# New issue orders for all five queues of a hybrid attention and DeltaNet layer

## The chip, the cores and the metric

The kernel runs on one core of one Trainium2 chip. The metric is the device time of one execution in microseconds (us), lower is better. Five engines work side by side and each takes its instructions strictly in order: TensorE (PE in the profile, PEld for its weight loads), VectorE (DVE), ScalarE (ACT), GpSimd (POOL) and SyncE (SP), which here does nothing but issue DMA transfers. POOL issues a few transfers too.

## What is computed

One layer of a diffusion backbone: 512 latent tokens and 256 context tokens, width 1024. Cut to what matters:

```python
hx = modulate(rms_norm(x), sh1, sc1); hc = modulate(rms_norm(ctx), csh1, csc1)
ak_x, av_x, qkv_x, db_x, da_x, aq_x, z_x, gate_x = split_cols(hx @ w_in)   # 512 tokens
ak_c, av_c, qkv_c, db_c, da_c = split_cols(hc @ w_in[:, :CTX_COLS])        # 256 tokens
attn = latent_attention(rope(norm(aq_x)), [k_c; k_x], [v_c; v_x])          # 8 heads, 768 keys
gdn  = gated_delta_net(silu(conv3(qkv)), decays, betas)   # 8 heads, both directions, chunked scan,
                                                          # a triangular solve in every chunk
y = (sigmoid(g_a) * (attn @ w_pa) + sigmoid(g_d) * (gdn @ w_pd)) @ w_out
x = x + g1 * y
x = x + g2 * (silu(g) * val) @ w_down   # g, val = conv3(modulate(rms_norm(x)) @ w_up)
return rms_norm(x, final_norm_w)
```

The modulations (sh1, sc1, g1, sh2, sc2, g2) are a vector times the 1024x6144 matrix w_mod.

## The kernel before

Every large product is made with three matmuls: each operand is split into a high part (rounded to fp32r) and a low part (what is left), and high x high, low x high and high x low are summed in one PSUM bank. ScalarE makes the high part of a weight tile (`whi<-wraw`), VectorE the low part (`wlo<-wraw,whi`); the raw tile (`wraw`, two buffers) comes from HBM by a transfer that SyncE issues. A column of a projection is 128 output channels: 8 x 3 matmuls into one of two banks called `mb` (`mc` in the second half of the kernel).

The work runs in this order. To about 53 us: the first modulations and norms. To 145 us: the projections for attention (`pq`). To 300 us: the attention, with projection columns of the DeltaNet woven between. From 300 to 729 us: the DeltaNet, head pair by head pair (four pairs), with more projection columns, and later the columns of w_pa and w_pd, woven in as filling; small matmuls of the scan write banks called `pb`. From 729 to 780 us the columns of w_pd alone, then w_out, and from about 830 us the MLP (`mc`).

For each head pair there is a triangular solve, 31 steps of two instructions (`prod<-X,R` and `R<-R,prod`), on VectorE for the first pair and on GpSimd for the other three; its result is transposed by VectorE into two tiles, `o_tr` and `o_nt`. The scan of a pair multiplies masks `M` (loaded as `M<-gamdr`, a constant added by GpSimd as `M<-M,cst`, then `M<-pqk,M` on VectorE) with `dl` on PE (`pb<-dl,M`).

The columns of w_pa are finished by `finish_pa`. For each of the eight columns it does a load, a multiplication and a store, through two buffers:

```python
def finish_pa(c, pa):
    ga = atA.tile([P, 512], F32, name="ga", tag="gt", bufs=2)
    SP.dma_start(ga, tdr[c])
    stt(ga, ga, 1.0, pa, ALU.add, ALU.mult)
    SP.dma_start(tdr[c], ga)
```

So the load of column c can be issued only when the store of column c-2 has landed, the multiplication waits for that load and for the column's bank `pa` (one of the two `mb`), and the bank is free for another column after the multiplication. The first two columns of w_pd take the two banks next; they read the DeltaNet's heads (`g_s`, `g_n`, `g_k`, `g_m`), of which four are reloaded (`sz<-gdr`) and split again. In the same stretch `late_mods` loads 24 rows of w_mod on GpSimd's queue into two buffers (`wl<-in_w_mod_dram`, 512 KB each), and VectorE multiplies each (`wl<-wl,cw`).

Every instruction of the kernel is recorded by one helper (line 275), which gives it a number in the order in which the program makes it, one count for each engine. At the end one string for each engine (`V_ORDER` for VectorE, `A_ORDER` ScalarE, `G_ORDER` GpSimd, `S_ORDER` SyncE, `T_ORDER` PE) lays down the order in which the queue holds them:

```python
def arrange(self, text):
    to = []
    for part in text.split():
        a, _, b = part.partition("-")
        to += [self.made[i].ins for i in range(int(a), int(b or a) + 1)]
    for a, b in zip(to, to[1:]):
        tc.add_manual_dep(b, a.name, ...)     # b stays behind a in its queue
```

An entry such as `1036 1038-1041` stands for five instructions. The waits between engines follow from the tiles that are read and written and are not laid down by the strings. These entries are spoken of below:

- SyncE: loads of `ga`, columns 4 to 7: 224, 227, 230, 233; stores `tdr<-ga`, columns 2 to 5: 217, 222, 225, 228; `sz<-gdr`: 214, 215, 219, 220; w_pa's last column of weights: 232; w_pd's first and second: 235, 236.
- VectorE: the multiplications of `ga`, columns 2 to 7: 1109, 1128, 1144, 1164, 1182, 1203; `g_s<-sz,g_s`: 1107, 1102; `wl<-wl,cw`: 1132; the low part of the weights for column 5 of w_pa: 1145; the last three R steps of the first pair's solve: 627, 629, 631, with `prod` 628, 630; the bank reads `t<-mb,col,t` behind them: 659, 660; `o_nt` of the second pair: 787, two of the `t<-mb,col,t` before it: 805, 806; a `KL<-pt,KH` of the attention's keys: 171.
- ScalarE: four copies out of a transposed bank, `co<-xb,hk`: 416 to 419; four copies `C<-NN`: 411 to 414; an exponential of the attention, `pm<-pS`: 253; a `whi<-wraw`: 315; a `TTm<-pb`: 503.
- GpSimd: the copy `TTm<-o_tr` 293 and the row load `wl<-in_w_mod_dram` 298.
- PE: the transposes `pt<-cst,qt` 634 and 635; the scores `pS<-KH,QH` 1454; `pb<-vtok,TTm` 2670; the first matmul of w_pd's second column, 4431.

Of the kernel before, what the change touches and what calls it, by code (L numbers as in the profile page):

```python
# [70 lines left out]
V_ORDER = ('2 6 5 0-1 3-4 7-65 70 66 71 67-68 72 75-76 78 77 73 79-80 82 74 83-84 81 120 69 85 92 86 91 87 93 89 '  # L71
           '88 94 90 95 100 96 102-103 97 99 98 104 101 105 121 111 122 106 112-114 124 107 115-116 125 117 123 '
           '128 119 108-110 126-127 130-131 129 136-137 118 134-135 132-133 139 138 187 141 158 142 159-161 165 '
           '162 166 163 167-169 188 164 143-145 170-176 178 146-148 179 177 149-150 222 180-183 151 190 184 152 '
           '191-192 140 189 153-155 193 156 194 185 157 223 197-198 186 195 199-202 196 204-205 203 220 214 '
           '206-208 255 215 209 211-212 210 213 224 216-219 256 225 232 226-230 287 233-234 240-241 235-237 221 '
           '231 242-244 238 245-248 305 249 253 250-251 336 239 252 257-259 265 260-261 254 262-263 266-268 272 '
           '269 273 271 274-276 264 277 270 279-284 347 278 288-289 285 295 286 296 354 297 290 292 291 306-307 '
           '298 293-294 300 299 313 308 314 301 309 302-303 311 310 312 315 304 319-320 317 316 321 318 322 327 '
           '368 328 324-326 329 323 337-338 385 330-331 339 343 333 332 334 340 344 341 335 342 345 400 350-351 '  # L80
           '346 394 405 348 352 359-360 349 357 353 358 361 355 362 369-370 356 436 371 364 363 372 365-366 '
           '375-376 374 367 373 377-378 431 381-382 380 443 379 450 383 390-391 384 388-389 386-387 401 392-393 '
           '402 395-398 403 408-410 399 404 407 414 406 415 464 412 411 413 422 481 423 420 424 416-417 419 418 '
           '421 432-433 425-426 434 427-428 439 429 440 435 496 437 430 446-447 441 438 442 444-445 448-449 '
           '455-456 453 452 490 454 457 451 465 458-459 466 501 460 467-468 461-462 471-472 470 463 469 477 475 '
           '473 478 474 553 479 531 476 486-487 484 480 483 488 485 482 497 489 498 491-492 499 493-494 504-505 '
           '500 562 502 506 495 510 503 508 511-512 509 507 518-519 516-517 514 513 515 520 527-528 522 521 529 '
           '523 530 524 534-535 532-533 525 536-539 638 540-541 526 542-543 546 550 548 547 674 678 672 544 549 '
           '545 551 671 679 552 675-676 673 677 680 797-798 792 927 793 554-555 794 556-557 799-800 795-796 '
           '559-560 558 644 561 563 567 566 564-565 633-634 568-569 650 635-636 570-576 637 577 639-640 578-583 '  # L90
           '641-642 584-588 643 589 656 590-591 645-646 592-595 647-648 596-601 649 662 602-604 651-652 605-607 '
           '653-654 608-611 668 612 655 613-617 657-658 618-627 659 628-631 660-661 663-664 632 670 666-667 665 '
           '683 692 669 681-682 704 685 688-689 684 687 690 708 832 693 930 934 691 694 932 928 933 686 696 931 '
           '935 695 697 699-700 698 801 703 701 716 702 709 705 710 706 726 711-713 929 714 707 740 717 833 721 '
           '719 718 715 720 727 729 728 722 730 723-724 731 734 756 732-733 735-736 741 725 737 743 742 744-745 '
           '776 748 746 739 747 749-750 738 757 751 758 958 752 759-760 753 761 766 808 764 762 767-768 765 763 '
           '769 754 770 777 755 771 779 773-774 778 780 772 782 815 783 785 959 775 784 788-789 805-806 791 781 '
           '786-787 790 936 823 802 834 803-804 809 812 835 813 807 811 810 814 831 817 836 840 816 818 839 841 '
           '837 843 845 838 842 844 819 824 820-821 852 826-827 1073 822 1072 825 828-830 846-847 863 849 848 '
           '854 853 855-857 850 858 876 859 864 860 851 862 866 861 868-869 867 865 870 889 871 873-874 872 875 '  # L100
           '879 877 880-882 906 878 883 886 884-885 887 916 888 892 890 894-895 893 891 896 901 899 897-898 904 '
           '902-903 900 907 905 911 910 908 912-914 909 917 940 920 915 918 923 919 924 921 925 922 926 946 '
           '937-939 942 960-961 957 945 941 944 948 943 962 967 947 963 966 968 950 949 970 953 951 965 969 971 '
           '954 972 952 964 981 1186 955-956 1187 973 977-978 974 979 975 980 992 976 982-984 1001 985 988 986 '
           '990 989 991 994 1018 993 987 995-997 999 1002 998 1004 1003 1005 1037 1000 1006 1009 1007-1008 '
           '1010-1011 1019 1021 1020 1012 1022 1055 1023 1013 1024 1028 1026 1029 1031 1030 1025 1032 1027 1042 '
           '1035 1014 1047 1036 1038-1041 1048 1016 1043 1033 1044 1034 1045-1046 1060 1015 1049-1052 1054 1053 '
           '1068 1017 1056-1057 1069 1074-1075 1061 1059 1058 1076 1062 1079 1094 1077-1078 1080 1063-1064 1081 '
           '1070 1084-1085 1065 1083 1066 1071 1086 1067 1087-1088 1092 1082 1110 1091 1098 1100 1089 1101 1099 '
           '1095 1093 1129 1097 1090 1103 1105-1106 1104 1109 1108 1115 1117-1118 1116 1114 1111 1145 1112 1120 '  # L110
           '1123 1126 1096 1121-1122 1124-1125 1128 1132-1135 1130 1136 1143 1165 1131 1137 1140 1148 1138-1139 '
           '1146 1141-1142 1153 1144 1149-1151 1107 1152 1147 1170 1183 1175 1154 1159 1102 1155 1160 1156 1162 '
           '1127 1163 1157-1158 1200 1161 1168 1201 1113 1171-1174 1119 1169 1176 1210 1164 1177-1178 1180 1166 '
           '1179 1181 1167 1204 1218 1185 1184 1223 1182 1205 1202 1188-1189 1203 1228 1190 1192 1195 1191 1194 '
           '1193 1197 1199 1196 1198 1217 1206 1208 1207 1209 1211-1212 1238 1213 1222 1214 1233 1219 1227 1215 '
           '1232 1216 1239 1220 1244 1224-1225 1229 1245 1237 1230 1221 1243 1226 1249 1231 1234 1240 1235 1241 '
           '1253 1246 1236 1247 1242 1248 1257 1250-1251 1261 1252 1265 1254 1256 1258 1255 1269-1270 1260 1262 '
           '1259 1263 1271 1301 1266 1274 1267 1264 1272 1268 1302 1273 1275-1277 1303 1278 1281-1282 1279 1283 '
           '1280 1285 1284 1287 1289 1286 1288 1300 1290-1291 1299 1293 1295 1292 1336 1297 1294 1304 1298 1296 '
           '1305-1307 1309 1311 1308 1310 1313 1312 1315 1314 1317 1316 1319 1321 1354 1318 1320 1322 1353 1331 '  # L120
           '1337 1323-1324 1372 1371 1340 1329 1325 1330 1345 1348 1326-1328 1332 1338 1333-1334 1341 1355 1390 '
           '1335 1339 1342-1343 1389 1346 1358 1347 1363 1349 1344 1350 1356-1357 1366 1351 1359 1352 1373 1360 '
           '1376 1364 1361 1407 1365 1362 1408 1381 1367-1369 1384 1370 1374-1375 1377 1391 1378-1380 1382 1394 '
           '1383 1420 1399 1402 1392 1385-1386 1393 1387-1388 1409 1395-1397 1400 1398 1412 1401 1417 1410 '
           '1403-1405 1421 1413 1411 1406 1426 1414-1415 1429 1422 1416 1418 1434 1437 1423 1427 1419 1424 1428 '
           '1442 1425 1435 1445 1430-1432 1450 1438 1436 1439 1433 1440 1443 1453 1444 1446-1448 1458 1461 1441 '
           '1451-1452 1466 1454 1449 1455 1459 1469 1456 1460 1462-1464 1457 1474 1477 1467 1465 1468 1482 '
           '1470-1471 1475 1485 1472 1476 1473 1478 1490 1479-1480 1493 1481 1483 1498 1484 1491 1486 1501 1492 '
           '1487-1489 1506 1494-1495 1507 1496 1499 1502 1500 1508 1497 1503-1504 1513-1514 1505 1509-1510 1515 '
           '1511-1512 1520-1521 1516 1522 1527 1518 1528 1519 1517 1529 1523 1525 1534 1524 1530 1526 1535-1536 '  # L130
           '1541 1531-1533 1537 1542 1539 1538 1543 1548-1549 1544-1545 1550 1555 1546 1556 1540 1547 1557 '
           '1551-1552 1558 1553 1559-1560 1554 1561-1567 1570 1568-1569 1571-1581')
# [1803 lines left out]
```

## Time and profile before

| what | value |
|---|---|
| time, median of three runs | 1207.3 us (1206.34, 1207.3, 1210.89) |
| the profiled execution's own time | 1203.08 us |
| its span, first to last instruction | 1201.3 us |
| mean granted TensorE clock | 0.993 of full speed |
| PE busy | 1172.9 us |
| DVE, ACT, POOL busy | 820.8, 591.4, 257.8 us |
| DMA moved | 174.96 MB, mean 146 GB/s |

Busy time of PE counts overlapping matmuls once. A matmul is drawn longer than the pace at which matmuls follow each other, so that an engine can be drawn busy through a short wait; the idle times given are lower bounds. The clock is given as a share of full speed, 2.4 GHz; 0.5 is 1.2 GHz.

### The profile page before, as it was taken

The numbers are of one execution on the slowest core, as the hardware profiler recorded it, in microseconds if no ns is written. First come the engines' busy times: TensorE is split into PE (matmuls) and PEld (weight loads), VectorE is DVE, ScalarE is ACT, GpSimd is POOL, SyncE is SP. The second block draws the span as 40 slices with busy tenths as digits, with TensorE's granted clock in tenths as the row PEclk, the third lists the DMA queues.
The fourth block names the chain that finished last, engine by engine and source line by source line (L and its number), as shares of the span: only waits on it lengthen the run. The fifth ranks groups of instructions, "written<-read, shape, count | busy, mean of one in ns | idle before, by whom it ended". The sixth has DMA issues, their size and how long they took to land.

```text
span 1201.3 us, 20365 instructions
## 1 busy us (share of the span) xinstructions
PE 1172.9 (98%) x7781; PEld 1012.9 (84%) x7781; DVE 820.8 (68%) x1614; ACT 591.4 (49%) x1372; POOL 257.8 (21%) x333
## 2 busy tenths in 40 slices
PE   9999999999998999999999998999999999999996
PEld 6899989999887888898887786889888888888886
DVE  4758798788798868856576896657676566563233
ACT  3535588777566756735446423334444444342231
POOL 0211100101304686784663111000000000000000
PEclk9999999999999999999999998999999999999998
DMA  9423333232444535435347777653433232333332
GB/s 380 155 96 102 109 92 125 69 112 86 186 170 147 179 113 182 169 107 190 129 139 244 254 258 262 230 185 107 158 140 105 88 106 89 105 97 97 97 97 70
DMA packets 57633, 174.96 MB, mean 146 GB/s; under 512 B 6240, under 2 KB 8768, under 8 KB 56128
## 3 DMA queue, kind: packets, MB, share of 16 engines
q1 hardware_dynamic: 54080, 161.08, 39.2%
q0 software_dynamic: 3456, 12.58, 3.2%
q8 instruction: 61, 1.00, 0.4%
q14 instruction: 36, 0.29, 0.1%
HBM read 146.85 MB, written 26.79 MB: 145 GB/s over the span
## 4 chain that ended last, share of the span: by engine, by line
PE 82%; DVE 9%; DMA 4%; issue 3%; POOL 1%; ACT 1%; SPq 0%; POOLq 0%; DVEq 0%; ACTq 0%
PE mc L275 34%; PE mb L275 24%; PE pb L275 7%; PE pq L275 6%; PE ab L275 4%; PE pS L275 3%; PE pm L275 2%; PE xb L275 1%; DVE R L275 1%; DVE t L275 1%; DMA tdr<-ga 1%; DVE wlo L275 1%; DMA wl<-in_w_mod_dram 1%; DVE prod L275 1%; PE pt L275 1%
## 5 line engine op out<-in xcount | busy, mean ns | idle before, releaser
L275 DVE TENSOR_TENSOR wlo<-wraw,whi 128x1024 fp32r<-128x1024 f32 (+3 forms) x155 | 188.6, 1220 | 104.1 <-ACT whi L275 103.3
L275 ACT ACTIVATE whi<-wraw 128x1024 fp32r<-128x1024 f32 (+3 forms) x155 | 159.2, 1030 | 177.2 <-PE mc L275 93.9
L275 PE MATMUL mc<-h,whi 128*128 128x512 f32 (+1 forms) x752 | 219.3, 376 | 0.0
L275 PE MATMUL mb<-hxH,whi 128*128 128x512 f32 x384 | 162.0, 422 | 3.3 <-DVE t L275 3.3
L275 PEld LDWEIGHTS mc<-h,whi 128*128 128x128 f32 x752 | 138.0, 188 | 25.4
L275 PE MATMUL mb<-hxH,wlo 128*128 128x512 f32 x384 | 151.7, 395 | 0.1
L275 PE MATMUL mb<-hxL,whi 128*128 128x512 f32 x384 | 149.7, 393 | 0.0
L275 PE MATMUL mc<-h,wlo 128*128 128x512 f32 (+1 forms) x376 | 141.2, 376 | 0.0
L275 PE MATMUL mc<-a,whi 128*128 128x512 f32 (+1 forms) x396 | 111.0, 366 | 0.6 <-DVE x L275 0.6
L275 POOL TENSOR_TENSOR rc<-rc,mhalf 128x2 f32<-128x2 f32 x4 | 3.0, 745 | 437.3 <-DVE rc L275 437.3
L275 PEld LDWEIGHTS mb<-hxH,whi 128*128 128x128 f32 x384 | 72.8, 190 | 17.7 <-DVE t L275 3.4
L275 PEld LDWEIGHTS mb<-hxH,wlo 128*128 128x128 f32 x384 | 72.4, 189 | 16.9 <-issue 0.6
L275 DVE SCALAR_TENSOR_TENSOR u<-mc,col,u 128x511 f32<-128x511 f32 x88 | 64.3, 745 | 28.1 <-ACT u L275 27.7
L275 PEld LDWEIGHTS mc<-a,whi 128*128 128x128 f32 x396 | 71.6, 189 | 12.8 <-DVE x L275 0.8
L275 PEld LDWEIGHTS mb<-hxL,whi 128*128 128x128 f32 x384 | 72.9, 190 | 11.1 <-DVE hxL L275 0.5
L275 PEld LDWEIGHTS mc<-h,wlo 128*128 128x128 f32 x376 | 70.8, 188 | 12.9
L275 PE MATMUL mc<-a,wlo 128*128 128x512 f32 (+1 forms) x198 | 72.4, 365 | 0.0
L275 POOL TENSOR_TENSOR prod<-X,R 128x31 f32<-128x31 f32 (+15 forms) x93 | 55.4, 596 | 21.8 <-DVE f L275 12.7
L275 ACT ACTIVATE u<-mc,col 128x512 f32<-128x512 f32 x44 | 33.7, 772 | 46.5 <-PE mc L275 35.1
L275 DVE SCALAR_TENSOR_TENSOR t<-mb,col,t 128x511 f32<-128x511 f32 (+1 forms) x76 | 49.0, 646 | 9.9 <-ACT t L275 9.0
L275 PE MATMUL pq<-whi,hxH 128*128 128x256 f32 (+1 forms) x192 | 55.4, 289 | 0.0
L275 POOL TENSOR_TENSOR R<-R,prod 128x31 f32<-128x31 f32 (+15 forms) x93 | 53.7, 577 | 6.9
(322 smaller groups left out, 2747.5 us busy)
## 6 DMA issues: line engine op xcount, KB each, us to landing
wraw<-in_w_cm_dram SPq DMA_DIRECT2D x48, 512.0 KB, 3.8
wraw<-in_w_up_dram SPq DMA_DIRECT2D x44, 512.0 KB, 3.3
wl<-in_w_mod_dram POOLq DMA_DIRECT2D x24, 512.0 KB, 4.6
wm<-in_w_mod_dram SPq DMA_DIRECT2D x8, 1024.0 KB, 13.4
wraw<-in_w_down_dram SPq DMA_DIRECT2D x16, 512.0 KB, 3.6
wraw<-in_w_aq_dram SPq DMA_DIRECT2D x10, 512.0 KB, 3.5
M<-gamdr SPq DMA_DIRECT2D x8, 512.0 KB, 6.6
wraw<-in_w_pa_dram SPq DMA_DIRECT2D x8, 512.0 KB, 4.5
```

What stands on the lines that cost most here:

```text
L275: self.made.append(fn(*a, **k))
```

## The change

No instruction, tile or transfer is added or removed. The five strings are replaced by other permutations of the same numbers. From the first place that differs to the last, the strings rule the stretch from 53 to 899 us of the profiled execution. Counted by the smallest set of entries that would have to be taken out and put back elsewhere, 490 of VectorE's 1582 entries move, 380 of ScalarE's 1182, 49 of GpSimd's 329, 103 of SyncE's 358 and 944 of PE's 6638 (mostly in groups of three, one k-step). No entry of SyncE stands more than 9 places from where it stood, none of VectorE more than 29.

The lines of the strings that hold the entries above, before and after:

```diff
 S_ORDER
-'214-215 217 232 224 219-220 222 227 235 237 225 238 230 236 228 233 243 231 246 234 249 239-242 244 '
+'229 217 215 232 224 235 222 225 219 227 220 236 230 228 237-238 233 243 231 246 234 239 241 240 249 '
...
 V_ORDER
-'162 166 163 167-169 188 164 143-145 170-176 178 146-148 179 177 149-150 222 180-183 151 190 184 152 '
+'222 146-147 182-183 148 171 149-151 184 152 190 153 191 189 185 223 192 154 156 193-194 155 197 195 '
...
-'653-654 608-611 668 612 655 613-617 657-658 618-627 659 628-631 660-661 663-664 632 670 666-667 665 '
+'652 605-607 653-654 608-609 668 610-611 655 612-615 657 616 658 617-629 659-661 663-664 630 670 '
...
-'769 754 770 777 755 771 779 773-774 778 780 772 782 815 783 785 959 775 784 788-789 805-806 791 781 '
-'786-787 790 936 823 802 834 803-804 809 812 835 813 807 811 810 814 831 817 836 840 816 818 839 841 '
+'781 786 791 787 823 805 803 802 804 806 834 813 835 807 936 809 811 810 812 816 831 817 837 844 814 '
...
-'1095 1093 1129 1097 1090 1103 1105-1106 1104 1109 1108 1115 1117-1118 1116 1114 1111 1145 1112 1120 '
-'1123 1126 1096 1121-1122 1124-1125 1128 1132-1135 1130 1136 1143 1165 1131 1137 1140 1148 1138-1139 '
+'1124 1130 1125 1132 1145 1128 1133 1135 1134 1136 1143 1131 1137 1165 1138 1140 1148 1139 1146 '
...
-'1127 1163 1157-1158 1200 1161 1168 1201 1113 1171-1174 1119 1169 1176 1210 1164 1177-1178 1180 1166 '
+'1156-1157 1162-1163 1161 1158 1200 1168 1171-1173 1166 1174 1164 1201 1113 1176 1169 1167 1119 1210 '
...
 A_ORDER
-'315 237 239 244 253 251 317 250 318-319 298 252 325 257 264 324 259 238 258 260-261 270 262-263 277 '
+'317 310 237 315 251 239 325 244 253 298 324 238 319 250 252 257 264 259-261 258 262 270 263 277 269 '
...
-'391-393 384 394-395 397-408 432 409 413 411-412 415 414 416-419 602 601 443 423 420 597 421 424 600 '
+'388 390 375 391 376 392 384 393-395 397-406 408 432 409 407 411-413 416 415 417-418 414 419 602 420 '
...
-'494 535 500 498 501 507 505 502 504 510 503 508 511 506 595 541 593 603 536 512 538 513 537 606 539 '
+'491 519 492 496-497 488 493-494 528 495 500 535 498 486 504 501 508 505 507 506 502 511 595 510 541 '
+'503 605 593 592 536 596 538 537 512 591 513-514 606 539 533 515 604 607 553 594 563 542 540 516 534 '
...
 G_ORDER
-'294 289-290 292 291 295 299-300 296 301 297-298 293 302-313 315-321 314 322-328')
+'222-285 289 294 290 293 291 295 299-300 292 301 297 296 298 302-313 315-320 314 321-328')
...
 T_ORDER
-'4413-4430 4434-4436 4440-4442 4431-4433 4437-4439 4447-4449 4443-4446 4450-4456 4460-4462 4457-4459 '
+'4389-4391 4409-4412 4408 4402-4404 4413-4430 4434-4436 4440-4442 4450-4452 4460-4462 4431-4433 '
```

## Rows read from the trace of the kernel before

**Rows 1.** The page: its first line, and the line with each engine's busy time, share of the span and instructions.

```profile
span 1201.3 us, 20365 instructions
...
PE 1172.9 (98%) x7781; PEld 1012.9 (84%) x7781; DVE 820.8 (68%) x1614; ACT 591.4 (49%) x1372; POOL 257.8 (21%) x333
```

**Rows 2.** Busy time by stretch: the stretch and its length in us, then PE, PEld, DVE, ACT and POOL busy us (instructions), the granted clock, the mean busy share of the 16 DMA engines, and GB/s.

```profile
53.00:300.00 247.00, 246.01 (x1809) 231.25 (x1808) 194.89 (x476) 162.08 (x467) 29.97 (x22) 1.00 0.30 101
...
650.00:729.00 79.00, 75.96 (x492) 64.09 (x491) 66.32 (x146) 28.10 (x61) 13.52 (x23) 1.00 0.80 265
729.00:741.00 12.00, 7.59 (x27) 5.81 (x25) 7.02 (x19) 3.71 (x18) 2.26 (x2) 0.72 0.79 273
...
780.00:900.00 120.00, 119.92 (x679) 105.39 (x679) 82.67 (x136) 50.55 (x78) 1.58 (x2) 1.00 0.43 150
...
368.50:372.00 3.50, 3.28 (x8) 2.65 (x9) 2.51 (x5) 2.91 (x5) 0.00 (x0) 0.54 0.13 51
734.00:741.00 7.00, 6.34 (x21) 5.10 (x21) 5.35 (x15) 1.54 (x2) 0.59 (x1) 0.55 0.76 268
```

**Rows 3.** The waits of PE over the whole span: what waited and for what, us in total, times, the longest.

```profile
PE mb L275 <- DVE ga L275: 4.4, 1, 4.4
PE mb L275 <- DVE t L275: 3.3, 3, 2.9
PE pb L275 <- issue: 2.1, 3, 1.2
PE xb L275 <- ACT co L275: 1.5, 1, 1.5
...
PE pb L275 <- POOL TTm L275: 1.0, 1, 1.0
...
PE pb L275 <- DVE o_nt L275: 0.7, 1, 0.7
PE pb L275 <- DVE dl L275: 0.6, 2, 0.5
```

**Rows 4.** PE in order of time around its longest wait: start, us, instruction, in brackets the idle time before it and what ended it.

```profile
729.86 0.40 PE L275 MATMUL mb<-g_s,wlo 128*128 128x512 f32 x1
734.66 1.19 PE L275 MATMUL mb<-g_s,whi 128*128 128x512 f32 x2 [4.41 <-DVE ga L275]
```

**Rows 5.** SyncE's issues in order of time, from 704 to 729 us: start, us in the queue, the transfer. In the order of the rows these are 219 and 220, 222, 227, 230, 228 and 233.

```profile
704.31 5.56 SPq L275 DMA_DIRECT2D sz<-gdr  x2
709.92 0.43 SPq L275 DMA_DIRECT2D tdr<-ga  x1
715.09 0.32 SPq L275 DMA_DIRECT2D ga<-tdr  x1
...
722.42 0.32 SPq L275 DMA_DIRECT2D ga<-tdr  x1
...
723.32 1.61 SPq L275 DMA_DIRECT2D tdr<-ga  x1
728.35 0.32 SPq L275 DMA_DIRECT2D ga<-tdr  x1
```

**Rows 6.** VectorE in order of time: the multiplications of `ga` for columns 3, 4 and 7.

```profile
691.40 0.68 DVE L275 SCALAR_TENSOR_TENSOR ga<-ga,mb 128x512 f32<-128x512 f32 x1
...
702.18 0.68 DVE L275 SCALAR_TENSOR_TENSOR ga<-ga,mb 128x512 f32<-128x512 f32 x1
...
733.83 0.69 DVE L275 SCALAR_TENSOR_TENSOR ga<-ga,mb 128x512 f32<-128x512 f32 x1 [2.26 <-DMA ga<-tdr]
```

**Rows 7.** VectorE and GpSimd in order of time, 362 to 368 us: the end of the first pair's solve and GpSimd's first mask.

```profile
362.03 0.28 DVE L275 TENSOR_TENSOR R<-R,prod 128x112 f32<-128x112 f32 x1
...
362.42 2.44 POOL L275 TENSOR_TENSOR M<-M,cst 128x1024 f32<-128x1024 f32 x1 [4.61 <-DVE R L275]
362.62 2.35 DVE L275 TENSOR_TENSOR R<-R,prod 128x87 f32<-128x87 f32 x1
...
365.52 2.29 DVE L275 TENSOR_TENSOR R<-R,prod 128x60 f32<-128x60 f32 x1
```

**Rows 8.** GpSimd in order of time, 660 to 662 us.

```profile
660.28 0.55 POOL L275 DMA_DIRECT2D wl<-in_w_mod_dram  x1 [8.69 <-DVE cw L275]
660.82 1.18 POOL L275 COPY TTm<-o_tr 32x384 f32<-32x384 f32 x1
```

**Rows 9.** Three results and the PE instructions that need them or their place, in order of time: VectorE's `KL<-pt` 171 and PE's `pt<-cst,qt` 634, which writes that `pt`; ScalarE's exponential `pm<-pS` 253 and PE's `pS<-KH,QH` 1454, which writes that `pS`; ScalarE's `TTm<-pb` 510 and 503 (the second of the two in the row) and PE's `pb<-vtok,TTm` 2670, which reads 503's.

```profile
98.41 0.42 DVE L275 TENSOR_TENSOR KL<-pt,KH 128x256 fp32r<-128x256 f32 x1
...
104.30 0.60 PE L275 MATMUL pt<-cst,qt 128*128 128x128 f32 x4
...
214.09 0.99 ACT L275 ACTIVATE pm<-pS,mx,qsc 128x768 f32<-128x768 f32 x1 [0.15 <-DVE mx L275]
...
215.75 0.40 PE L275 MATMUL pS<-KH,QH 128*128 128x512 f32 x1
...
398.89 0.97 ACT L275 ACTIVATE TTm<-pb 64x384 f32<-64x384 f32 x2
...
403.25 0.61 PE L275 MATMUL pb<-vtok,TTm 128*128 128x128 f32 x4
```

**Rows 10.** Transfers by kind: count, KB each, median us from issue to landing. The row is that of GpSimd's queue.

```profile
wl<-in_w_mod_dram POOLq DMA_DIRECT2D x24, 512.0 KB, 4.6
```

More of the change, by code (lines that the diff above doesn't have):

```diff
@@ L68 @@
 AQ, AK, AM, AR = 24, 10, 32, 10
-V_ORDER = ('2 6 5 0-1 3-4 7-65 70 66 71 67-68 72 75-76 78 77 73 79-80 82 74 83-84 81 120 69 85 92 86 91 87 93 89 '
[56 rows of a table removed]
+V_ORDER = ('2 6 5 0-1 3-4 7-65 70 66 71 67 75 68 72 76 73 78 77 79-80 120 74 82 81 91-92 83-84 93 85-86 94 87-88 '
[57 rows of a table added]
            '1470-1471 1475 1485 1472 1476 1473 1478 1490 1479-1480 1493 1481 1483 1498 1484 1491 1486 1501 1492 '
@@ L132 @@
            '1551-1552 1558 1553 1559-1560 1554 1561-1567 1570 1568-1569 1571-1581')
-A_ORDER = ('0-32 34 33 36-37 68 39-40 35 41-42 54 38 43-44 46 45 47-50 55 51-53 56 58 57 60 59 61 64-65 63 62 67 '
[43 rows of a table removed]
-G_ORDER = ('0-9 11-12 10 13-14 16 15 17-20 22 24 28 25-27 30 29 21 32 35 23 33 36 123 37 31 34 41 39 117-118 46 '
[4 rows of a table removed]
-S_ORDER = ('0-18 21 24 22-23 25-26 19-20 27-32 34-36 38 41 33 47 54 42 44 37 39 57 40 49-50 52 63 43 45 58-59 61 '
[9 rows of a table removed]
-T_ORDER = ('0-244 260-262 245-259 263-304 308-315 305-307 316-321 334-335 322-333 336-361 386-387 362-385 '
[63 rows of a table removed]
+A_ORDER = ('0-32 34 33 36-37 68 39-40 54 35 38 41-44 46-48 45 49-50 55-57 51-53 58 60 59 61 64 62 65 63 69 82 '
[44 rows of a table added]
+G_ORDER = ('0-9 11 10 12 14 13 15-20 22 24 26 25 21 28 23 27 35 29-30 33 36-37 32 34 123 41 39 31 117-118 43 42 '
[4 rows of a table added]
+S_ORDER = ('0-18 21 24 22-23 25-28 20 29-31 19 32 34-36 38 41 33 47 42 54 44 37 39 50 49 52 40 57 63 45 58 43 59 '
[9 rows of a table added]
+T_ORDER = ('0-309 334-335 310-333 336-353 362-364 354-361 386-387 365-385 388-414 436-438 415-435 439-471 '
[81 rows of a table added]
 C_ID, C_ONE, C_MS, C_MI, C_TRI = 0, 128, 256, 512, 768
```

345 rows, old and new, of tables (A_ORDER, G_ORDER, S_ORDER, T_ORDER) are left out of this document.

## Prediction, made before the change was run

> **What bounds the kernel now.** First the page: PE is busy 1172.9 of 1201.3 us [rows 1], so a new order can win 28.4 us of idle time at the most, and what a slow clock costs; no other engine comes near. Then busy time by stretch, to see where those 28.4 us lie [rows 2]. From 53 to 300 us PE idles 1.0 us, from 780 to 900 us 0.1 us; there an order can only lose. From 650 to 729 us it idles 3.0 us and from 729 to 741 us 4.4 us. The clock column says more: 0.54 over the 3.5 us from 368.5 and 0.55 over the 7 us from 734. A mean of 0.55 is 6.3 us at 1.2 GHz and the rest at 2.4 GHz; PE does half its work in them and loses 3.15 us. From 368.5 it loses 1.6 us in the same way. Both stretches follow a long wait of PE, so each of these two waits costs more than its idle time.
>
> Then the waits of PE by what ended them [rows 3]. The two longest are 4.4 us for the multiplication of `ga` and 2.9 us (of 3.3) for a `t`. Behind them come 1.5 us for ScalarE's `co`, 1.0 for a copy by GpSimd, 0.7 for `o_nt`, 0.6 for `dl`, and 2.1 us in three pauses that no semaphore explains. So two places hold 7.3 us of idle time and 4.75 us of slow clock, 12 us in all; what is left is in small pieces.
>
> **The longest wait, followed back.** PE stops at the first matmul of w_pd's second column, 4431, for 4.41 us [rows 4]. The bank is freed by column 7's multiplication, 1203, which VectorE starts at 733.83 after idling for its load [rows 6]. That load, 233, was issued at 728.35: it needs the buffer of column 5, whose store, 228, was issued at 723.32, behind the load 230 at 722.42 [rows 5]. The load of column 5, 227, came at 715.09 because its buffer belongs to column 3, whose store, 222, was issued at 709.92. But column 3 had been multiplied at 691.40 [rows 6]. The store sat in SyncE's queue for about 18 us behind 219 and 220, which wait for VectorE to empty the tiles that they reload (704.31, and 5.56 us for the pair). A queue held in order is the cause, and the string is what can change it.
>
> **The change, part by part.**
>
> *SyncE around 700 us.* After the change the stores 222 and 225 stand ahead of 219 and 220, behind the weight load 235. Column 4 is multiplied at 702.18 and 0.68 us later its store can go [rows 6]; 222, for the earlier column, goes before it. The load 235 needs a raw tile that is free once column 6's weights are split; I assume that this is done by 703, well ahead of column 6. So both stores go by about 703.5, and 227 follows them and 219 (704.31) instead of following 222's landing from 709.92: from the row, 715.09 - 709.92 = 5.2 us from store to next load, so about 704.5 or, if 222 goes only at 703, 708. That is 7 to 10 us earlier. The load 230 follows 225's landing by about 709 instead of 722.42, and 228 and 233, one round on, gain about as much. 4.4 us are enough for the wait to go, since column 7's own matmuls end before w_pd's begin, and 4431 now also stands one group of six matmuls later. Then PE does not stop and the clock has no cause to fall: -(4.4 + 3.15) = -7.55. Bounds: 0 if the chain does not come earlier, -7.55. I take -7.5, the upper end, since the gain of the chain is nearly twice what is needed. What is late next: the loads of `gd` and `ga` for w_pd, which follow the last store; they too come earlier by the same chain.
>
> *VectorE and GpSimd at 362 to 369 us.* GpSimd's `M<-M,cst` runs 2.44 us from 362.42, and the R step that starts at 362.62 takes 2.35 us, to the same end; the R step before took 0.28 with a larger tile [rows 7]. The next, from 365.52, takes 2.29. The bank reads 659 and 660 stand among them and PE waits for 660. In the new order both stand behind the second slow R step 629 and ahead of 630 and 631, so 660 ends where it did, within 0.4 us, and neither mask is moved. I take 0; bounds 0 and -(2.9 + 1.6) = -4.5 if the masks happen to land elsewhere.
>
> On this pair the Trainium skill (SBUF — State Buffer, "Who interferes with whom") says that a VectorE instruction with two SBUF inputs and a GpSimd instruction that reads SBUF share a port which one of them holds for its whole length while the other is blocked. The trace agrees (2.35 against 0.28 us). By that rule the time is not won back by moving 659 between the two R steps or behind them, and the term is 0; without it both R steps would be short and the term -4.5.
>
> *The small waits.* GpSimd's copy 293 ran at 660.82 behind the row load 298, which had kept the queue idle for 8.69 us [rows 8]; now it stands ahead of 298. PE's 1.0 us for it goes: -1.0. The `co` copies 416 to 418 now stand ahead of one of the `C<-NN` and a `t`: -1.2 of 1.5. `o_nt` 787 stands ahead of 805 and 806, which it followed: -0.7. The low-part split 1145, which stood ahead of `dl` that PE waits for, now follows: -0.6, and about -0.2 for what hangs on them. Sum -3.7; bounds 0 and -4. For the three pauses without a releaser the profile shows no wait that could be taken away: 0.
>
> *What the new order makes late.* Nothing shows a wait that does not exist yet, so this is bounded from margins. `KL<-pt` 171 ends at 98.83 and PE's 634 needs its place at 104.30, a margin of 5.5 us; 171 now stands 17 places later in VectorE's queue. The exponential 253 ends at 215.08, 0.67 us ahead of PE's 1454, and stands 4 places later, behind a `whi` (315). `TTm` 503 ends at 399.86, 3.4 us ahead of PE's 2670, and stands 5 places later, behind a `whi` too [rows 9]. Hundreds of others move too. I take 1 us for each of the three and 1 us for all the others: +4.0. Bounds: 0, since idle time of VectorE and ScalarE may take it up, and +8, twice that, about the 0.7 to 1.5 us of the small waits of today [rows 3] at eight places.
>
> **The sum:** -7.5 + 0 - 3.7 + 4.0 = -7.2. The profiled execution took 1203.08 us, 1.8 more than its span and 4.2 less than the median of the three runs, a little below the lowest of them (1206.34). So a profile of the new kernel would show about 1196, and against the median it is 1207.3 - 7.2 = 1200.1 us.
>
> **The rivals.** 0.5% of the time is 6.0 us, about what a measurement of this kernel can tell from no change: faster is below 1201.3, slower above 1213.3.
>
> A, the chain is bound by the transfers and not by their order. For it: from 650 to 729 us the DMA engines are 0.80 busy, at 265 GB/s, and 0.79 behind it [rows 2]; stores and loads of `ga` run beside the 24 row loads of GpSimd's queue, each 4.6 us to landing [rows 10]. Against it: the store 222 stood in the queue unissued; no transfer was slow. If it holds, the 4.4 us and the slow clock stay: -3.7 + 4.0 = +0.3, 1207.6. On this the Trainium skill (DMA: Bandwidth & Descriptors, "Issuing engines are not separate DMA queues") says that transfers of all issuing engines run on the same 16 DMA engines and interleave. By that rule, stores issued earlier meet the row loads and land later, which is this rival; no row of this kernel shows a transfer made slow by another alone.
>
> B, the waits move elsewhere. PE stops today where the place in a queue holds it and not the work, and a new order can have such places of its own. If new waits reach 9 us and not 4, the sum is -7.5 - 3.7 + 9 = -2.2, 1205.1. For it: the number of entries that move, and margins such as 0.67 us. Against it: from 53 to 300 us even today's order hides all but 1.0 us.
>
> C, on the other side: VectorE's queue is tied to GpSimd's row loads. The low part of column 5's weights, 1145, now stands behind `wl<-wl,cw` 1132, which waits for a row load; the weight load 232 on SyncE waits for 1145, and 224, 235, 222 and 225 stand behind 232. Two row loads late, 2 x 4.6 us [rows 10], stop PE for 9.2 us in w_pa; the clock falls for 3.15 us as it did at 734, the stores come no earlier, so the 7.5 us are not won: 9.2 + 3.15 + 0.3 = +12.65, 1219.9. It is slower by over 6.0 from a delay of 2.6 us on. Against it: 1132 stands beside column 3's multiplication in both strings, so near 691, and column 5's matmuls come after column 4's, which is multiplied at 702.18 [rows 6].
>
> **How the numbers follow.** The forecast 0.58 (0.51 of it below 1201.3, 0.07 above), A 0.16, B 0.16, C 0.10. So faster 0.51, the same 0.39, slower 0.10. The likeliest case has its own range of 1195.6 (the wait at 365 us gone too) to 1204.1 (all new waits at twice the size). The range for 8 in 10 reaches up over A and B to 1209; down, with no new wait at all, it is 1196.1, with the wait at 365 us gone as well 1191.6, and I cut it at 1193. C is left out above, a little below.
>
> **What would show it.** Right: in the waits of PE the row for `ga` is gone or below 0.5 us, no clock below 1 from 720 to 741 us, the store of column 3 issued before 705 us, the row for GpSimd's `TTm` gone, the wait for `t` near 368 still 2 to 3 us. Rival A: the store is issued early and its load still lands near 733. B: new rows of 0.5 to 2 us in the waits of PE, at `pt`, `pS` or `pb`. C: PE waits for `wlo` or for w_pa's weights at about 695 us. I am wrong if PE's idle time is not smaller by about 4 us at 730, or if it is and comes back from 53 to 300 us.

## The result, and the profile after

The changed kernel takes 1197.6 us (median of seven runs, 1193.0 to 1200.2), the kernel before beside it 1204.1 us (1200.7 to 1210.9): 6.5 us less. The ratio, here and below taken over all runs and not from the two medians, is 0.994, with an interval from 0.991 to 0.997, or 7.6 us less. In a second comparison (the run after_again below) the ratio is 0.995 (0.993 to 0.997), 6.3 us less. The profiled execution of the new kernel took 1197.6 us, 5.5 less than that of before; the prediction had -7.2.

The page of the new kernel, its first line and that of the engines, answers to [rows 1].

```profile
span 1195.8 us, 20328 instructions
...
PE 1168.6 (98%) x7781; PEld 1010.2 (84%) x7781; DVE 816.9 (68%) x1614; ACT 589.3 (49%) x1372; POOL 254.9 (21%) x333
```

PE idles 27.2 us where it idled 28.4: only 1.2 us less. The other 4.3 us are busy time: the same matmuls ran more of their time at the full clock, as the rows of 729 to 741 us and of 368.5 to 372 us below show. The waits of PE by what ended them, as [rows 3]:

```profile
PE mb L295 <- DVE t L295: 4.1, 2, 3.1
PE pb L295 <- DVE S L295: 2.4, 1, 2.4
PE pb L295 <- issue: 1.8, 2, 1.0
PE pb L295 <- ACT TTm L295: 1.7, 3, 1.0
PE mb L295 <- DVE ga L295: 1.6, 1, 1.6
...
PE pS L295 <- DVE qtmp L295: 1.0, 1, 1.0
...
PE xb L295 <- ACT co L295: 0.6, 2, 0.5
...
PE pb L295 <- DVE o_nt L295: 0.3, 1, 0.3
```

`ga` went from 4.4 to 1.6 us; the rows for GpSimd's `TTm` and for `dl` are gone; `S`, ScalarE's `TTm` and `qtmp` are new or larger. By stretch, with the columns of [rows 2]:

```profile
53.00:300.00 247.00, 245.28 (x1794) 229.79 (x1793) 192.37 (x473) 160.52 (x467) 28.09 (x24) 1.00 0.30 98
...
650.00:729.00 79.00, 73.76 (x505) 63.33 (x504) 66.92 (x146) 30.85 (x76) 11.75 (x22) 1.00 0.80 265
729.00:741.00 12.00, 11.85 (x56) 9.47 (x56) 10.02 (x24) 4.05 (x9) 3.61 (x3) 1.00 0.84 291
...
368.50:372.00 3.50, 3.08 (x14) 2.56 (x15) 1.32 (x3) 3.11 (x9) 0.00 (x0) 1.00 0.21 82
```

From 729 to 741 us PE is busy for 11.85 us at a clock of 1.00, where it was 7.59 at 0.72. From 650 to 729 us it now idles 5.2 us, not 3.0. SyncE's issues in order of time, to be held beside [rows 5]; in the order of the rows they are 235, 222 with 225, 219, 227, 230, 228 and 233:

```profile
698.02 0.33 SPq L295 DMA_DIRECT2D wraw<-in_w_pd_dram  x1
698.45 5.52 SPq L295 DMA_DIRECT2D tdr<-ga  x2
704.77 0.32 SPq L295 DMA_DIRECT2D sz<-gdr  x1
705.14 0.49 SPq L295 DMA_DIRECT2D ga<-tdr  x1
...
710.90 0.43 SPq L295 DMA_DIRECT2D ga<-tdr  x1
716.17 0.32 SPq L295 DMA_DIRECT2D tdr<-ga  x1
...
719.89 0.42 SPq L295 DMA_DIRECT2D ga<-tdr  x1
```

The store of column 3 goes out at 698.45 instead of 709.92, and the load of column 7, which PE waited for, at 719.89 instead of 728.35. What PE still waits for at that place is VectorE's queue; VectorE, then PE, in order of time:

```profile
723.75 1.23 DVE L295 SCALAR_TENSOR_TENSOR wl<-wl,cw 128x1024 f32<-128x1024 f32 x1 [1.75 <-DMA wl<-in_w_mod_dram]
...
725.31 2.35 DVE L295 TENSOR_TENSOR wlo<-wraw,whi 128x1024 fp32r<-128x1024 f32 x2
727.58 0.42 DVE L295 TENSOR_TENSOR oacc<-oacc,pb 128x256 f32<-128x256 f32 x1
727.91 0.68 DVE L295 SCALAR_TENSOR_TENSOR ga<-ga,mb 128x512 f32<-128x512 f32 x1
...
728.74 0.71 PE L295 MATMUL mb<-g_s,whi 128*128 128x512 f32 x2 [1.65 <-DVE ga L295]
```

The multiplication of column 6 (1182) now stands behind a `wl` that waits 1.75 us for its row load, and behind two splits. Its own load was issued at 710.90. The same happens at 668.96: a `wl` (1086) waits 2.69 us for a row load, `S<-pb` (1087) stands behind it, and PE waits 2.37 us for `S`:

```profile
667.22 1.23 DVE L295 SCALAR_TENSOR_TENSOR wl<-wl,cw 128x1024 f32<-128x1024 f32 x1 [2.69 <-DMA wl<-in_w_mod_dram]
...
668.48 0.42 DVE L295 TENSOR_SCALAR S<-pb 128x256 f32<-128x256 f32 x1
668.96 0.71 PE L295 MATMUL pb<-S,kT 128*128 128x128 f32 x4 [2.37 <-DVE S L295]
```

At 365 us the wait for `t` is there as before. GpSimd's two masks, VectorE's two steps beside them (628 and 629) and PE, to be held beside [rows 7]:

```profile
363.08 4.71 POOL L295 TENSOR_TENSOR M<-M,cst 128x1024 f32<-128x1024 f32 x2
363.16 2.40 DVE L295 TENSOR_TENSOR prod<-X,R 128x60 f32<-128x60 f32 x1
365.59 2.27 DVE L295 TENSOR_TENSOR R<-R,prod 128x60 f32<-128x60 f32 x1
...
368.92 0.47 PE L295 MATMUL mb<-hxH,whi 128*128 128x512 f32 x1 [3.09 <-DVE t L295]
```

### The profile page after: what moved, and what is told of

Read it like the earlier page. It is cut to its first block, busy times and chain, and to the rows that moved or that the text cites. A ratio compares the mean times of both kernels' runs of the same rounds, so it can differ in the third digit from the quotient of the medians.

```text
span 1195.8 us, 20328 instructions
## 1 busy us (share of the span) xinstructions
PE 1168.6 (98%) x7781; PEld 1010.2 (84%) x7781; DVE 816.9 (68%) x1614; ACT 589.3 (49%) x1372; POOL 254.9 (21%) x333
## 4 chain that ended last, share of the span: by engine, by line
PE 59%; issue 4%; DVE 3%; DMA 2%; POOL 1%; ACT 0%; POOLq 0%; DVEq 0%; ACTq 0%
PE mc L295 34%; PE mb L295 16%; PE pb L295 7%; DMA wl<-in_w_mod_dram 1%; PE pk L295 1%; DMA cw<-in_rows_dram 0%; POOL wl L295 0%; DVE wlo L295 0%; PE pqk L295 0%; DMA ga<-tdr 0%; DVE wl L295 0%; DVE C L295 0%; PE xb L295 0%; DVE oacc L295 0%; POOL f L295 0%
## 5 line engine op out<-in xcount | busy, mean ns | idle before, releaser
L295 POOL TENSOR_TENSOR R<-R,prod 128x31 f32<-128x31 f32 (+15 forms) x93 | 56.7, 609 | 6.7
```

Of the source, the lines that this page charges most:

```text
L295: self.made.append(fn(*a, **k))
```

## The experiments

The name of each run stands in brackets behind its heading. Ratios are to the kernel before, run beside it.

**The stores alone.** (stores_alone) The kernel before, with one stretch of SyncE's string replaced:

```diff
-'214-215 217 232 224 219-220 222 227 235 237 225 238 230 236 228 233 243 231 ...
+'214-215 217 232 224 235 222 225 219 227 220 236 230 228 237-238 233 243 231 ...
```

> The kernel before, with one stretch of SyncE's string in the new order: 235 222 225 219 227 220 236 230 228 237 238 233 243 in place of 219 220 222 227 235 237 225 238 230 236 228 233 243. Nothing else moves. Theory (the store of column 3 stuck behind 219 and 220 makes the 4.41 us wait, and the wait the slow clock): store 222 is issued near 698 to 703 us, the load of column 7 near 720 instead of 728.35, PE does not wait for `ga` (below 0.5 us), no clock below 1 from 729 to 741 us, and the time falls by 7.5 us, ratio to the kernel before about 0.994. Rival A (the transfers bound the chain): the load of column 7 still lands near 733, the wait stays at 4 us, ratio 1.000. Rival: the new order of VectorE or PE is needed for it: half of the wait stays, ratio about 0.997.

Measured: 1198.4 against 1202.4 us (medians, 4.0 us apart), ratio 0.9954 (0.9933 to 0.9974), by the ratio 5.5 us less. The wait for `ga` is gone and so is the slow clock. Busy time from 729 to 741 us:

```profile
729.00:741.00 12.00, 12.00 (x58) 9.79 (x58) 9.31 (x23) 4.97 (x6) 0.90 (x2) 1.00 0.86 325
```

SyncE's issue of column 7's load, 4.9 us earlier than in [rows 5]:

```profile
723.48 0.32 SPq L275 DMA_DIRECT2D ga<-tdr  x1
```

Rival A falls: a new order of 13 entries of one queue (7 of them moved, counted as in the section on the change) makes the chain come in time, with the DMA engines as busy as before. The third expectation, half of the wait, falls with it. The 7.5 us are an upper end; the interval reaches from 3.1 to 8.1 us. In this profile `dl` rose to 2.4 us (0.6 before) and `r` to 0.8 (0.2), so the next waits may have taken back some of what the stores give; how much one profile does not show, since `dl` was 1.2 and 1.4 us in two other profiles with the old order of the stores (copy_first and burst_cut).

**The stores undone.** (stores_undone) The kernel after, with the old order in that stretch alone:

```diff
-'229 217 215 232 224 235 222 225 219 227 220 236 230 228 237-238 233 243 231 ...
+'229 217 215 232 224 219-220 222 227 235 237 225 238 230 236 228 233 243 231 ...
```

> The kernel after, with the same stretch of SyncE's string in the old order, all other strings new. Theory (the stores are the gain): a wait for `ga` of 4 to 5 us and a slow clock come back near 730 us where the kernel after has 1.65 us and none, +2.8 us of wait and up to +3.15 us of clock: the gain over the kernel before shrinks from 7.6 to 2 us or less, ratio 0.998 to 1.000. Rival (the gain is the sum of the many small moves in the other strings): ratio stays at 0.994, the wait for `ga` below 2 us.

Measured: 1210.8 us, ratio 1.0061 (1.0039 to 1.0083): 7.3 us slower than before, far beyond what was expected. In order of time SyncE's 219 and 220, 222 and 227, then VectorE's and PE's waits:

```profile
707.13 5.01 SPq L295 DMA_DIRECT2D sz<-gdr  x2
712.19 0.42 SPq L295 DMA_DIRECT2D tdr<-ga  x1
719.12 0.32 SPq L295 DMA_DIRECT2D ga<-tdr  x1
...
722.68 0.69 DVE L295 SCALAR_TENSOR_TENSOR ga<-ga,mb 128x512 f32<-128x512 f32 x1 [4.96 <-DMA ga<-tdr]
...
723.43 0.73 PE L295 MATMUL mb<-at,whi 128*128 128x512 f32 x2 [2.40 <-DVE ga L295]
726.63 1.22 PE L295 MATMUL pb<-S,qT 128*128 128x128 f32 x4 [2.23 <-DVE dl L295]
743.77 1.19 PE L295 MATMUL mb<-g_s,whi 128*128 128x512 f32 x2 [6.69 <-DVE ga L295]
```

219 and 220 go out 2.8 us later than before, the store behind them at 712.19 instead of 709.92, and the load of column 5 at 719.12 instead of 715.09. VectorE stands still for it for 4.96 us, in an order in which `dl` comes behind column 5. So PE pays three times (2.4, 2.2 and 6.7 us), and the clock is 0.88 from 729 to 741 us and 0.91 from 741 to 780. (This profile is of the slowest of the six executions, 1214.0 us, and also holds a pause of 3.0 us near 555 us, of which more below.) The new order of SyncE is worth 5.5 us in the old company and 14 to 15 in the new (1.0061 less 0.9948 or 0.9937).

**`t` ahead of the masks.** (t_first) The kernel after, with VectorE's 659 and 660 ahead of step 625:

```diff
-'... 618 617-629 659-661 663-664 630 670 '
+'... 618 617-624 659-660 625-629 661 663-664 630 670 '
```

> The kernel after, with VectorE's bank reads `t` 659 and 660 moved ahead of the solve's step 625, so that they run near 362.1 us, ahead of the two instructions that GpSimd's masks hold for 2.4 us each. Theory (the wait of PE at 365 us is only the place of these two in VectorE's queue): PE's wait for `t` falls from 3.1 us to 0, the solve ends about 1 us later, which nothing waits for, and the time falls by 3 us: ratio to the kernel before about 0.991. Rival (the solve is what PE waits for next): a new wait of 1 to 3 us for the solve's results between 370 and 385 us takes the gain, ratio 0.994.

Measured: 1195.3 us, ratio 0.9921 (0.9897 to 0.9945), not to be told from the kernel after by time; the interval holds both expectations. In the profile the wait of 3.1 us is gone, and ScalarE's `co` near 374 rose from 0.5 to 1.25 us: 0.8 of the 3.1 came back. The masks still hold two of VectorE's steps (2.34 and 2.35 us), now behind the reads.

**The masks earlier.** (masks_earlier) The kernel after, with GpSimd's 117 and 118 ahead of the memset 31:

```diff
-'... 123 41 39 31 117-118 43 42 46 ...
+'... 123 41 39 117-118 31 43 42 46 ...
```

> The kernel after, with GpSimd's masks 117 and 118 (`M<-M,cst`) moved ahead of the memset 31, so that they start near 360.4 us instead of 363.1. Theory (VectorE's two-input steps in SBUF stand still while a GpSimd instruction reads SBUF, and a memset, which reads nothing, does not hold them): two steps of the solve from about 360.4 take 2.3 to 2.4 us each, 628 and 629 take 0.19 to 0.25 us instead of 2.40 and 2.27, the memset runs beside short steps, and PE's wait for `t` stays at 3.1 us, since the same 4.5 us are lost ahead of it. Rival (the last steps are slow for their own shape or their place): 628 and 629 stay at 2.3 us wherever the masks are.

One run, 1192.6 us, which tells nothing of the time. VectorE's steps, GpSimd's masks and the memset in order of time:

```profile
360.76 2.46 DVE L295 TENSOR_TENSOR prod<-X,R 128x156 f32<-128x156 f32 x1
363.25 2.41 DVE L295 TENSOR_TENSOR R<-R,prod 128x156 f32<-128x156 f32 x1
365.69 0.30 DVE L295 TENSOR_TENSOR prod<-X,R 128x135 f32<-128x135 f32 x1
...
367.80 0.22 DVE L295 TENSOR_TENSOR R<-R,prod 128x60 f32<-128x60 f32 x1
...
360.64 4.84 POOL L295 TENSOR_TENSOR M<-M,cst 128x1024 f32<-128x1024 f32 x2
365.42 2.66 POOL L295 MEMSET TTm<- 128x3072 f32 x1
```

The long steps go with the masks: 156 elements take 2.4 us beside a mask, and 60, which took 2.27 in the kernel after, take 0.22 beside the memset. PE's wait for `t` is 3.08 us as before. The Trainium skill (SBUF — State Buffer, "Who interferes with whom") says that a VectorE instruction with two SBUF inputs contends with a GpSimd instruction that reads SBUF and not with one that only writes it; the rows agree on both halves.

**The kernel after once more.** (after_again)

> The kernel after, unchanged, beside the kernels of the same batch. Theory: ratio to the kernel before 0.993 to 0.995. In the profile the waits whose releaser is named come back at the same places (`t` 3.1 us at 365, `S` 2.4 at 669, `ga` 1.6 at 728.7, within 0.5 us each); what changes from one execution to the next is the pause without a releaser near 556 us (0.2 to 3.3 us in the six profiles so far) and whether the clock falls behind the wait at 365. Rival: the named waits differ by more than 1 us from execution to execution, and then no single profile can tell a gain of 1 us.

Measured: 1197.6 against 1204.3 us, ratio 0.9948 (0.9929 to 0.9967); the profiled span is 1192.8 us, 3.0 less than in the first profile of the same kernel. Its waits of PE:

```profile
PE mb L295 <- DVE t L295: 4.2, 2, 3.1
...
PE mb L295 <- DVE co L295: 1.3, 1, 1.3
...
PE pb L295 <- DVE S L295: 1.1, 1, 1.1
PE pS L295 <- DVE qtmp L295: 1.0, 1, 1.0
```

`t` and `qtmp`, which hang on engines alone, repeat to 0.1 us. `S` is 1.1 instead of 2.4 us, `ga` has no row, and near 402 PE waits 1.3 us for `co`, where the first profile had 1.0 for `TTm`. The first two hang on when a row load lands: VectorE's waits for it ahead of `S` and of column 6 are 1.45 and 0.37 us here, 2.69 and 1.75 in the first profile. So the theory held for the time and for `t` and `qtmp`, and the rival for `S` and `ga`: where a transfer stands behind a wait, one profile gives it to about 1.5 us only.

**The waits of after taken away.** (mended) Five moves in VectorE's and ScalarE's strings:

```diff
 V_ORDER
-279 285 280 278 281-284
+279-283 278 284-285
-617-629 659-661
+617-624 659-660 625-629 661
-1086-1087 1067 1088
+1087-1088 1086 1067
-1181 1218 1202 1185 1204-1205 1184 1182
+1181-1182 1218 1202 1185 1204-1205 1184
 A_ORDER
-541 503                           +503 541
```

> The kernel after, with five waits that its trace shows taken away by moving what they wait for: VectorE's 659 and 660 ahead of 625 (3.1 us at 365); 1182, the multiplication of column 6, ahead of the multiplication 1218 that waits for its row load and of the two weight splits behind it (1.65 us at 728.7); 1087 and 1088 (`S<-pb`) ahead of 1086, which waits 2.7 us for its row load (2.4 us at 669); 280 to 283 ahead of 278 and 285 (1.0 us at 139.6, half of it); and ScalarE's `TTm` 503 ahead of the weight split 541, which waits 1.6 us for its raw tile (1.0 us at 403). Theory (a queue's head that waits for a transfer holds up what PE needs, and a place ahead of it costs nothing): -3.1 -1.65 -1.0 -0.5 and, at 669, about -0.8 of 2.4, since the load of `at` lands only at 667.2 there: -7.0 us against the kernel after, ratio to the kernel before about 0.988, PE idle about 20 us. Rival (the waits move on): each leaves a new wait of about half its size near it, -3.5 us, ratio 0.991.

Measured: 1193.4 us, ratio 0.9920 (0.9898 to 0.9943). By time the interval leaves out the theory's 0.988 and holds the rival's 0.991, and it overlaps that of the kernel after. PE idles 22.4 us (27.2 in the kernel after): between the two expectations. `S`, `ga` and ScalarE's `TTm` are gone or at 0.2 us. `co` (703) takes 1.3 us near 401, as in after_again, and `f` 1.1 us near 729, which PE did not wait for as long as it came there 5 us later.

**Four more.** (mended_more) On top of these, 703 ahead of 701, 633 and 634 ahead of 565, 1133 to 1136 ahead of 1145 (and of 1128, the multiplication of column 3, behind it), 1184 ahead of 1204:

> The kernel of the run called mended, with four more places on VectorE: `co<-tz,mb` 703 ahead of 701 (PE waits 1.3 us for it at 401), the bank reads `t` 633 and 634 ahead of the copy 565 (1.0 us at 322), the r steps 1133 to 1136 ahead of the weight split 1145 (0.7 us at 689), and `oacc` 1184 ahead of the weight splits 1204 and 1205 (1.1 us for `f` at 729). Theory: each of these waits goes, -4 us against mended, ratio to the kernel before about 0.988. Rival (what is moved back is needed as soon): two of the four come back as waits for what now stands behind, -2 us, ratio 0.990.

Measured: 1189.8 us, ratio 0.9890 (0.9866 to 0.9915): 1.1% faster than before, and its interval does not touch that of the kernel after beside it (0.9929 to 0.9967). The four waits went, but where 633 and 634 were moved, `xb` waits 1.7 us for VectorE's `co` near 329 instead of the 1.0, and near 695 PE waits 0.6 us for `M`. PE idles 22.8 us in this profile, no less than in that of mended, because the pause described next took 3.5. So this version beats the kernel before and the kernel after; that it beats mended, and which of 0.988 and 0.990 is right, the times do not show.

**The burst of small matmuls cut.** (spread, burst_cut) PE has a pause near 555 us that no semaphore explains, always near the end of the second of two bursts of 48 small matmuls (32 x 32; each is drawn as two). It was 1.2 us in the profile of before, 1.0 in that of after, and from 0.2 to 3.5 us in the others. In mended_more:

```profile
554.44 0.26 PE L295 MATMUL pb<-Y,o_tr 32*32 32x32 f32 x1 [3.54 <-issue]
```

The burst was cut, first on top of mended_more:

```diff
 T_ORDER
-3503-3555 3589-3592 3556-3558
+3503-3514 3553-3555 3515-3526 3556-3558 3527-3538 3551-3552 3539-3550 3589-3592
```

> The kernel of the run called mended_more, with PE's second burst of 48 small matmuls (32 x 32, near 552 us, 8 to 16 ns apart) cut into four groups of 12 with 6 large matmuls and two of `pk` between them; the same work in another order. Theory (the pause without a releaser near 555 us is PE's sequencer running dry on a burst of short instructions): the pause is below 0.3 us and the times scatter less; -1 us against mended_more. Rival (the pause has another cause, or the small matmuls' results are then late): the pause stays at 0.2 to 3 us, or a wait for `TTm` near 562 us of 1 to 2 us takes its place; 0.

Measured: 1190.3 us, ratio 0.9889 (0.9865 to 0.9914), the same as mended_more; with intervals of 5 us in all a gain of 1 us could not be seen. The pause is gone in its profile, where mended_more shows 3.5 us and a slow clock behind it. Busy time from 540 to 565 us in mended_more:

```profile
540.00:565.00 25.00, 21.46 (x285) 18.34 (x284) 13.38 (x22) 11.91 (x34) 12.79 (x14) 0.86 0.59 203
```

and in spread:

```profile
540.00:565.00 25.00, 24.81 (x352) 20.62 (x351) 17.54 (x32) 14.52 (x39) 12.64 (x14) 1.00 0.62 202
```

Then the same cut (without 3589 to 3592) in the kernel before:

> The kernel before, with PE's second burst of 48 small matmuls near 556 us cut into four groups of 12, as in the run called spread, and nothing else moved. Theory (the pause of 0.2 to 3.5 us at the end of that burst, mean 1.8 us over nine profiles, belongs to the burst): the pause is below 0.3 us; -1.5 us, and at times a slow clock less: ratio to the kernel before 0.997 to 0.999. Rival: the pause stays, or the results of the burst are then late and PE waits for `TTm` near 565 us as long: 1.000.

Measured: ratio 1.0014 (1.0000 to 1.0027). The pause is gone again, so the theory holds for the pause, and it fails for the time. There was less to win than the 1.5 us: in the three profiles with PE's old order and the burst uncut the pause was 1.19, 0.24 and 0.56 us (before, stores_alone, copy_first). And the burst ends later: from its first matmul to its last took 2.2 us before (from 555.34) and takes 3.6 us now (from 556.74), and `pk<-kT` waits 0.8 us for VectorE's `NN` near 567. That this wait comes from the later end is argued, not shown. Why PE stands still in the uncut burst stays open; no run shows that its sequencer runs dry.

**The copy first.** (copy_first) The kernel before, with GpSimd's 293 ahead of 298:

```diff
-'... 301 297-298 293 302-313 ...
+'... 301 297 293 298 302-313 ...
```

> The kernel before, with GpSimd's copy 293 ahead of the row load 298 and nothing else moved; it also serves as a second look at the kernel before. Theory: PE's wait of 1.0 us for GpSimd's `TTm` near 661 us is gone, and what PE needs next (the split `at`, whose load lands about 662.7) takes over less than half of it. All other waits of the kernel before are there again: `ga` 4.4 us near 734 with a clock near 0.55 behind it, `t` 2.9 us near 368. Rival for the copy: PE waits for `at` instead by the same 1.0 us. Rival for the clock: behind the same waits the clock stays at 1.00, as it did behind the wait for `t` in four of six profiles so far.

One run, 1204.4 us, within the times of the kernel before beside it (1200.9 to 1206.1). The row for GpSimd's `TTm` is gone, and PE waits for the split `at` at the same place. Of the waits of PE:

```profile
PE mb L275 <- DVE ga L275: 6.9, 2, 5.3
...
PE mb L275 <- ACT at L275: 0.9, 1, 0.9
```

Busy time from 368.5 us on, behind the wait for `t`:

```profile
368.50:372.00 3.50, 3.50 (x9) 2.77 (x10) 2.67 (x4) 3.04 (x6) 0.00 (x0) 0.54 0.23 90
```

In this one profile the rival was right: 0.9 of the 1.0 us came back as a wait for ScalarE's half of `at`, whose load lands late. The long waits of the kernel before are there again, with the slow clock behind each: `ga` at 5.3, 4.0 in the profile of burst_cut and 4.4 in the first.

## Why the prediction was right

The sum was -7.2, and the two comparisons gave -6.3 and -7.6, with intervals that reach together from -4.0 to -11.1. (The forecast time, 1200.1 us, was counted from three early runs with a median of 1207.3; from the 1204.1 of the seven it is 1196.9, and 1197.6 was measured.) By rows of the first two profiles, the terms were:

- *SyncE around 700 us* (predicted -7.5). The times of the chain were met within 2 us: 222 at 698.45 (before 703.5), 227 at 705.14 (704.5 to 708), 230 at 710.90 (709, where it missed most), column 7's load 8.5 us earlier (7 to 10). The clock's 3.15 us came. Of the wait 2.8 us came in the first profile, so that the sign set for it, a row for `ga` below 0.5 us, failed there (1.6); in the second all 4.4 came. The step "what is late next" was incomplete: it looked at loads, and it was VectorE's queue. With the old VectorE the stores alone give 5.5 (3.1 to 8.1).
- *VectorE and GpSimd at 365 us* (0). The wait stayed, 3.09 for 2.92 us, and the mechanism is shown by masks_earlier. But 1.6 us of slow clock went with no wait gone, which is luck of the execution. The step that failed is "each of these two waits costs more than its idle time": of the eight profiles that hold this wait (2.9 to 3.1 us), four show the slow clock behind it and four do not. So the 1.6 us were no sure cost of this wait.
- *The small waits* (-3.7). The rows fell by 1.0, 0.9 (`co`), 0.4 (`o_nt`) and 0.6 (`dl`), 2.9 in all. At the places meant it was more: `co` near 322 fell from 1.53 to 0.17 us (though of 416 to 418 only 416 passed the `t`) and `o_nt` near 466 from 0.66 to nothing, and new waits for a `co` near 375 (0.47) and an `o_nt` near 380 (0.30) stand in the same rows. But copy_first shows that the 1.0 for GpSimd's copy was not to be had alone, and behind `co` the bank read `t` near 322 took 1.0 us. The waits for `QL` and `at` went too, 1.8 us, which was not foreseen.
- *What the new order makes late* (+4.0, bounds 0 and +8). By rows it is +6.3: `S` +2.1, ScalarE's `TTm` +1.7, `qtmp` 1.0, `t` +0.8, `qt` 0.4, `r` +0.3. Of the three places named, one came: 503, at the 1 us given. `KL` and the exponential 253 cost nothing. The term was too small by half, and its places were mostly others.

The rows add up: -2.8 - 2.9 - 1.8 + 6.3 = -1.2 of idle time, as the page has it, and the two clock terms, 4.75 us by the rows of before, account for the 4.3 us of busy time. So the sum held in part by luck, because misses cancelled: on one side 2.3 us more of new waits and, in the first profile, 2.4 us less from the stores and the small waits; on the other 1.6 us of clock and 1.8 of waits that went unforeseen. In time, all the moves outside SyncE's stretch bring 1 to 2 us on top of it (0.9937 and 0.9948 against 0.9954 for the stretch alone), within the intervals; +0.3 had been predicted for them.

Of the rivals, A is refuted by stores_alone. The chain of `ga` came in time while the DMA engines were 0.82 busy from 650 to 729 us. The Trainium skill (DMA: Bandwidth & Descriptors, "Issuing engines are not separate DMA queues") says that the transfers of all engines interleave on the same engines; that such sharing moves the row loads by the 1.3 us by which they differ between two executions, no run here shows. B happened in part (the new waits were 6.3, not 9). C has the right mechanism at other places: VectorE stood behind row loads at 669 and 724, for 2.4 and 1.65 us of PE's time, not for 9.

## What to carry to other kernels

Where a transfer is late, look first at how long it stood in its queue and behind what: a store that was ready at 692 and left at 710 cost 4.4 us of waiting and 3 us of clock, and a new order of 13 entries of one queue won most (5.5 us of 6.3 to 7.6) of what nearly 2,000 moved entries won. Orders of different queues belong together: the same new orders without those 13 were 7 us slower than before. And a wait that is taken away shows the next one, so price it by what PE needs next and when that is ready, not by its own length (by the rows of one profile each, 1.0 us of a copy gave 0.1, and 3.1 us of `t` gave about 2.3).

## What the runs showed of the hardware that was not expected

- The clock behind a wait of PE of about 3 us is not settled by the wait: at the same place it was 0.54 in the profiles of before, copy_first and burst_cut, 0.72 in stores_undone, and 1.00 in four others. Behind waits of `ga` of 4.0 us and more it was low in all four profiles that have one, and behind the pauses of 3.0 to 3.5 us near 555 us in all three (0.83, 0.83 and 0.91 from 545 to 565 us).
- In the second of two bursts of 48 small matmuls near 555 us PE stands still for 0.2 to 3.5 us, differently from profile to profile (1.0 and 0.8 us in the two of after); the first burst, as long, shows no such pause. With the second cut into groups of 12, in two kernels, no pause of 0.2 us is left there. No gain shows in the times (0.9889 beside 0.9890, and 1.0014).
- A memset by GpSimd leaves VectorE's two-input steps at 0.22 to 0.34 us, and a mask that reads SBUF holds them for 2.3 to 2.5 us, whether they have 60 or 156 elements.
